# Weight pieces of three FFNs at many places in their tiles, and two FFNs with moving rows read and PSUM written from the end

## The chip, the cores and the metric

The kernel runs on one core of a Trainium2 chip. The metric is the time of one execution on the device in microseconds. The core has a matrix engine (TensorE: PE for matmuls, PEld for loading the stationary weights), a vector engine (DVE), a scalar engine (ACT), GpSimd (POOL), and a queue on SyncE (SP) from which the loads from memory are issued. Operands lie in SBUF, with 128 partitions; matmul results go to PSUM.

## What is computed

A two-layer encoder trunk on one sequence of 256 tokens with 1024 features in float32. Each layer is a half-step SwiGLU feed-forward (FFN), a mixing step of windowed attention and a convolution module with gates, a second half-step FFN, and a gated per-layer embedding:

```python
def swiglu(x, w_in, w_out):
    gate, up = jnp.split(x @ w_in, 2, axis=-1)
    return (jax.nn.silu(gate) * up) @ w_out

for i in range(DEPTH):                       # DEPTH = 2
    h = x + 0.5 * swiglu(rms_norm(x, norm_ffn1[i]), w_ffn1_in[i], w_ffn1_out[i])
    u = rms_norm(h, norm_mix[i])
    q, k, v, c, g = jnp.split(u @ w_in[i], splits, axis=-1)
    ...
    h = h + (g_attn * y_attn + g_conv * y_conv) @ w_o[i]
    h = h + 0.5 * swiglu(rms_norm(h, norm_ffn2[i]), w_ffn2_in[i], w_ffn2_out[i])
    x = h + (p[i] @ w_pe_proj[i]) * jax.nn.sigmoid(rms_norm(h, norm_pe[i]) @ w_pe_gate[i])
```

The FFN width is 2816, so `w_ffn*_in` is 1024 x 5632 and `w_ffn*_out` is 2816 x 1024. There are four FFNs; the text numbers them 0 and 1 (first and second of layer 0), 2 and 3 (first and second of layer 1).

## The kernel before

All activations are kept with features on the partitions and the 256 tokens along the free dimension: `x32` and the normed copies are 8 chunks of 128 features by 256 tokens, `h` in the FFN is 22 such chunks. A float32 product is made from three matmuls in a reduced format (float32r): each operand is split into a high and a low part, and high x high, high x low and low x high are accumulated in PSUM. That is the inner loop `mm3`: for each chunk of 128 features of the contraction there are three matmuls, with a 128 x 128 piece of the weights as stationary operand (`w_hi` or `w_lo`) and a 128 x 256 chunk of activations as moving operand.

An FFN first runs `gate_up` 22 times: two output blocks of 128 features (one of the gate, one of the up half), each from 8 chunks, into the PSUM tile `ps_gu`; then `down` 8 times, each from 22 chunks in three groups of 8, 7 and 7, into `ps_fo`. In the trace the operands are named after their tiles: `x0h`/`x0l` are the inputs of FFN 0, `xf0`, `xn0` and `xf1` those of FFNs 1, 2 and 3, and `h_hi`/`h_lo` the hidden rows of each.

The class `Weights` streams the weights in the order in which they are used. `spec` notes one piece, `load_upto` issues its load from memory into a ring of 5 `raw` tiles (8 KiB per partition), and `prep_upto` splits it: ACT copies the high part into a `w_hi` tile (L108) and DVE subtracts it from the raw values into `w_lo` (L109). There are 7 tiles of each, and 6 pieces are made ahead (`LOOK`). `get` hands out the next piece and advances the preparation. The order on each engine comes from a scheduler that reads the program in this order.

The tiles' addresses are set by the order of the pools and by small filler tiles:

```python
ROW = 64
G0, G1, G2 = 24, 16, 8
PLACE = 4
...
def rows(pool, k, name, **kw):
    t = pool.tile([P, k * T + ROW], F32R, name=name, **kw)
    return t[:, PLACE : PLACE + k * T].rearrange("p (k t) -> p k t", t=T)
```

With these the 4 KiB `w_hi` and `w_lo` tiles begin at multiples of 256 bytes within a partition (the first of them at 64768), and every tile of moving rows begins 112 bytes past one (`x0h` at 130400 + 16, `h_hi` at 162144 + 16). A piece of weights is a run of 128 elements for each chunk, 512 bytes apart; a chunk of rows is 1024 bytes. So in each FFN matmul the moving operand lies 112 bytes behind the stationary one, modulo 256.

Two small products of the mixing step, `keys_values` (`ps_kv`, L733 to L735) and `queries` (`ps_q`, L777 to L779), have the roles exchanged: 128 tokens of the rows are stationary and the weights move, 256 or 512 columns at a time. `attn_out` (`ps_ao`, L946) multiplies in full float32 from the raw tiles.

Of the kernel before, what the change touches and what calls it, by code (L numbers as in the profile page):

```python
# [10 lines left out]
F32R = mybir.dt.float32r  # L11
# [4 lines left out]
P = 128  # L16
T = 256
D = 1024
KD = D // P
# [4 lines left out]
QD = 512  # L24
CD = 512
KC = CD // P
# [6 lines left out]
NEG = -1e9  # L33
LOOK = 6
RAW_BUFS = 5
DMA_SCRATCH = 8192
BACKGROUND = 800
WEIGHTS_LAG = 100
ATTN = 7
# [2 lines left out]
ROW = 64  # L42
G0, G1, G2 = 24, 16, 8
PLACE = 4


class Weights:


# [2 lines left out]
    def __init__(self, tc, raw_pool, w_pool):  # L52
        self.tc, self.nc = tc, tc.nc
        self.raw_pool, self.w_pool = raw_pool, w_pool
        self.units, self.specs = [], []
        self.raw, self.ready, self.held, self.hooks = {}, {}, {}, []
        self.next_load = self.next_prep = self.next_get = 0
        self.behind = ()
        self.rest, self.pin, self.lag, self.parts = 0, None, 0, 1

    def unit(self, k, n, sources):
        self.units.append((k, n, sources))
        return len(self.units) - 1

    def spec(self, k, n, pieces):

        self.specs.append((k, n, pieces, False))

    def raw_spec(self, unit, k, c0, n):
        self.specs.append((k, n, [(unit, 0, c0, 0, n)], True))  # L70

    def limit(self):
        held = [p[0] for s in self.specs[self.next_get : self.next_prep] if s[3] for p in s[2]]
# [12 lines left out]
    def prep_upto(self, i):  # L86
        nc = self.nc
        while self.next_prep <= min(i, len(self.specs) - 1):
            k, n, pieces, as_is = self.specs[self.next_prep]
            for u, *_ in pieces:  # L90
                self.load_upto(u + RAW_BUFS - 2)
                if u >= self.next_load:
                    return
            if as_is:
                ((u, k0, s0, _, w),) = pieces
                self.ready[self.next_prep] = self.raw[u][:, k0 : k0 + k, s0 : s0 + w]
                self.next_prep += 1
                continue
            hi = self.w_pool.tile([P, KD * P], F32R, name="w_hi")
            lo = self.w_pool.tile([P, KD * P], F32R, name="w_lo")  # L100
            hv = hi[:, : k * n].rearrange("p (k n) -> p k n", n=n)
            lv = lo[:, : k * n].rearrange("p (k n) -> p k n", n=n)
            step = k // self.parts
            for a, (u, k0, s0, d0, w) in ((a, p) for a in range(0, k, step) for p in pieces):
                at = slice(a, a + step)
                src = self.raw[u][:, k0 + a : k0 + a + step, s0 : s0 + w]
                parts = (
                    nc.scalar.copy(out=hv[:, at, d0 : d0 + w], in_=src),  # L108
                    nc.vector.tensor_tensor(  # L109
                        out=lv[:, at, d0 : d0 + w],  # L110
                        in0=src,
                        in1=hv[:, at, d0 : d0 + w].bitcast(F32),
                        op=ALU.subtract,
                    ),
                )
                if self.pin:
                    for ins in parts:
                        self.pin(ins)
                    self.pin = None
            self.ready[self.next_prep] = (hv, lv)  # L120
            self.next_prep += 1
# [16 lines left out]
    def get(self):  # L138
        i = self.next_get
        due = [fn for at, fn in self.hooks if at <= i]  # L140
        self.hooks = [h for h in self.hooks if h[0] > i]
        for fn in due:
            fn()
        p0 = self.tc.cur_priority
        self.tc.cur_priority = p0 + self.lag
        with ExitStack() as queue:
            for ins in self.behind:
                queue.enter_context(self.tc.issue_after(ins))
            self.prep_upto(i + LOOK - self.rest)
        self.tc.cur_priority = p0  # L150
        self.next_get += 1
        return self.ready.pop(i)


@with_exitstack
def encoder_kernel(ctx: ExitStack, tc: tile.TileContext, a: dict, out: bass.AP):
    nc = tc.nc
# [71 lines left out]
    ws = Weights(tc, raw_pool, w_pool)  # L229
# [4 lines left out]
    def cols_unit(w, k, c0, n):  # L234
        return ws.unit(k, n, [(whole, w[: k * P, c0 : c0 + n].rearrange("(k p) n -> p k n", p=P))])

    def ffn_specs(w_in, w_out, quick=False):
        for j in range(KF // 2):
            if quick and j == 0:
                for c in range(2):  # L240
                    for c0 in (0, FF):
                        u = cols_unit(w_in, KD, c0 + c * P, P)
                        ws.spec(KD, P, [(u, 0, 0, 0, P)])
                continue
            ug = cols_unit(w_in, KD, j * 256, 256)
            uu = cols_unit(w_in, KD, FF + j * 256, 256)
            for c in range(2):
                ws.spec(KD, P, [(ug, 0, c * P, 0, P)])
                ws.spec(KD, P, [(uu, 0, c * P, 0, P)])
        for f in range(KD // 2):  # L250
            us = [
                ws.unit(n, 256, [(whole, w_out[k0 * P : (k0 + n) * P, f * 256 : (f + 1) * 256].rearrange("(k p) n -> p k n", p=P))])
                for k0, n in KGROUPS
            ]
            for c in range(2):
                for u, (_, n) in zip(us, KGROUPS):
                    ws.spec(n, P, [(u, 0, c * P, 0, P)])

    KGROUPS = [(0, 8), (8, 7), (15, 7)]

    def mix_specs(l):
        w = a["w_in"][l]
        c0 = QD + 2 * P

        def conv_specs(j, n):
            uv = cols_unit(w, KD, c0 + j * P, n * P)
            ug = cols_unit(w, KD, c0 + CD + j * P, n * P)
            for c in range(n):
                ws.spec(KD, P, [(uv, 0, c * P, 0, P)])
                ws.spec(KD, P, [(ug, 0, c * P, 0, P)])  # L270

        conv_specs(0, 2)
        ukv = cols_unit(w, KD, QD, 256)
        for i in range(2):
            ws.spec(KC, 256, [(ukv, i * KC, 0, 0, 256)])
        for i in range(2):
            uq = cols_unit(w[i * KC * P : (i + 1) * KC * P], KC, 0, QD)
            for k in range(0, KC, 2):
                ws.spec(2, QD, [(uq, k, 0, 0, QD)])
        conv_specs(2, 2)  # L280
        g0 = QD + 2 * P + 2 * CD
        for j in range(8):
            u = cols_unit(w, KD, g0 + j * 256, 256)
            for c in range(2):
                ws.spec(KD, P, [(u, 0, c * P, 0, P)])
        w = a["w_attn_out"][l]
        for j in range(2):
            src = w[:, j * 512 : (j + 1) * 512].rearrange("(v c p) n -> v p c n", v=2, p=HD)
            u = ws.unit(KC, 512, [
                (lambda v: v[0:HD], src[0]),  # L290
                (lambda v: v[HD : 2 * HD], src[1]),
            ])
            for c in range(2):
                ws.raw_spec(u, KC, c * 256, 256)
        w = a["w_conv_out"][l]
        for j in range(2):
            u = cols_unit(w, KC, j * 512, 512)
            for c in range(2):
                ws.spec(KC, 256, [(u, 0, c * 256, 0, 256)])
        w = a["w_o"][l]  # L300
        for j in range(4):
            u = cols_unit(w, KD, j * 256, 256)
            for c in range(2):
                ws.spec(KD, P, [(u, 0, c * P, 0, P)])

    def pe_specs(l):
        up = cols_unit(a["w_pe_proj"][l], 2, 0, 1024)
        for c in range(2):
            ws.spec(2, 512, [(up, 0, c * 512, 0, 512)])
        for j in range(4):  # L310
            u = cols_unit(a["w_pe_gate"][l], KD, j * 256, 256)
            for c in range(2):
                ws.spec(KD, P, [(u, 0, c * P, 0, P)])

    for l in range(L):
        ffn_specs(a["w_ffn1_in"][l], a["w_ffn1_out"][l], quick=l == 0)
        mix_specs(l)
        ffn_specs(a["w_ffn2_in"][l], a["w_ffn2_out"][l])
        pe_specs(l)


# [10 lines left out]
    def mm3(ps, w, x, first=True, last=True, k0=0, x_k0=0, n_k=None, cols=slice(0, P), pin=False):  # L332
        (wh, wl), (xh, xl) = w, x
        n_k = wh.shape[1] if n_k is None else n_k
        for k in range(n_k):
            kx = x_k0 + k
            f, e = first and k == 0, last and k == n_k - 1
            for wa, xa, a, b in ((wh, xh, f, False), (wh, xl, False, False), (wl, xh, False, e)):
                mm = nc.tensor.matmul(ps, wa[:, k0 + k, cols], xa[:, kx, :], start=a, stop=b)  # L339
                if pin:  # L340
                    tc.keep_in_program_order(mm)

# [153 lines left out]
    with tc.manual_schedule(engines={mybir.EngineType.Activation, mybir.EngineType.DVE}):  # L496
# [9 lines left out]
        for k in range(KD):  # L506
            if 2 <= k < 6:
                xT[k] = mm_tile("ps_xt")[:, :T]
            else:
                c0 = 0 if k < 2 else 512  # L510
# [712 lines left out]
```

## Time and profile before

| | us |
|---|---|
| median of 2 runs | 1093.14 |
| the runs | 1092.87, 1093.42 |
| the profiled execution | 1092.97 |
| its span, first to last instruction | 1091.2 |
| FFN 0, first ps_gu to last ps_fo | 9.7 to 192.5 |
| FFN 1 | 339.4 to 519.9 |
| FFN 2 | 547.6 to 727.7 |
| FFN 3 | 874.6 to 1055.2 |

The profiled execution is 1.8 us longer than its span, and 0.2 us under the median. In the page's rows a busy time is the union of an engine's instructions; matmuls overlap one another, so that the mean duration of one says little of how fast they follow each other. A view by tile gives minimum, median and maximum duration in ns, and the starts of the first and the last of a group in us. The granted clock of TensorE was 0.998 of full speed over the span.

### The profile page before, as it was taken

The numbers are of one execution on the slowest core, as the hardware profiler recorded it, in microseconds if no ns is written. First come the engines' busy times: TensorE is split into PE (matmuls) and PEld (weight loads), VectorE is DVE, ScalarE is ACT, GpSimd is POOL, SyncE is SP. The second block draws the span as 40 slices with busy tenths as digits, with TensorE's granted clock in tenths as the row PEclk, the third lists the DMA queues.
The fourth block names the chain that finished last, engine by engine and source line by source line (L and its number), as shares of the span: only waits on it lengthen the run. The fifth ranks groups of instructions, "written<-read, shape, count | busy, mean of one in ns | idle before, by whom it ended". The sixth has DMA issues, their size and how long they took to land.

```text
span 1091.2 us, 22048 instructions
## 1 busy us (share of the span) xinstructions
PE 1082.8 (99%) x9178; PEld 1061.2 (97%) x9178; DVE 822.0 (75%) x1229; ACT 621.0 (57%) x1040; POOL 84.5 (8%) x123
## 2 busy tenths in 40 slices
PE   9999999999999999999999999999999999999997
PEld 9999999999999999999999999999998999999997
DVE  6876666899989766666886666669999986666664
ACT  7655445676767555445765554557776665554552
POOL 2000001210002000001100000113100100000110
PEclk9999999999999999999999999999999999999999
DMA  9876556556066646546556564566634666564531
GB/s 310 281 250 220 179 166 226 177 170 178 15 230 231 220 166 219 182 167 232 185 177 216 171 210 148 186 229 195 154 117 139 212 200 216 172 207 148 188 115 39
DMA packets 195695, 203.01 MB, mean 186 GB/s; under 512 B 3731, under 2 KB 188899, under 8 KB 195596
## 3 DMA queue, kind: packets, MB, share of 16 engines
q1 hardware_dynamic: 195564, 201.60, 55.9%
q8 instruction: 72, 1.18, 0.4%
q14 instruction: 27, 0.22, 0.1%
q10 hardware_dynamic: 32, 0.01, 0.0%
HBM read 200.53 MB, written 1.06 MB: 185 GB/s over the span
## 4 chain that ended last, share of the span: by engine, by line
PE 92%; DVE 2%; ACT 2%; DMA 1%; issue 1%; POOL 0%; SPq 0%; DVEq 0%; ACTq 0%; POOLq 0%
PE ps_gu L339 41%; PE ps_fo L339 22%; PE ps_g L339 8%; PE ps_c L339 4%; PE ps_pe L339 4%; PE ps_wo L339 4%; PE ps_co L1049 2%; DMA raw<-in_w_ffn_in_dram 1%; DVE w_lo L109 1%; PE ps_pp L339 1%; PE ps_s L818 1%; ACT g L932 1%; PE ps_o L874 1%; PE ps_q L778 1%; PE ps_q L777 1%
## 5 line engine op out<-in xcount | busy, mean ns | idle before, releaser
L109 DVE TENSOR_TENSOR w_lo<-raw,w_hi 128x1024 fp32r<-128x1024 f32 (+2 forms) x377 | 450.9, 1202 | 199.3 <-ACT w_hi L108 199.3
L108 ACT CAST w_hi<-raw 128x1024 fp32r<-128x1024 f32 (+2 forms) x377 | 387.7, 1034 | 365.1 <-PE ps_gu L339 191.0
L339 PE MATMUL ps_fo<-h_hi,w_hi 128*128 128x256 f32 x704 | 193.0, 275 | 0.0
L339 PE MATMUL ps_fo<-h_lo,w_hi 128*128 128x256 f32 x704 | 193.0, 275 | 0.0
L339 PE MATMUL ps_fo<-h_hi,w_lo 128*128 128x256 f32 x704 | 193.0, 275 | 0.0
L339 PEld LDWEIGHTS ps_fo<-h_lo,w_hi 128*128 128x128 f32 x704 | 131.8, 188 | 0.0
L339 PEld LDWEIGHTS ps_fo<-h_hi,w_lo 128*128 128x128 f32 x704 | 131.8, 188 | 0.0
L339 PEld LDWEIGHTS ps_fo<-h_hi,w_hi 128*128 128x128 f32 x704 | 131.8, 188 | 0.0
L443 POOL TENSOR_TENSOR sq_acc<-sq_acc,sq 128x256 f32<-128x256 f32 x56 | 52.6, 939 | 829.2 <-ACT sq L442 828.8
L669 DVE SCALAR_TENSOR_TENSOR y<-cpad,cw,y 128x256 f32<-128x256 f32 x240 | 101.8, 487 | 0.1
L339 PE MATMUL ps_gu<-xf0l,w_hi 128*128 128x256 f32 x352 | 97.0, 276 | 0.0
L339 PE MATMUL ps_gu<-xf1l,w_hi 128*128 128x256 f32 x352 | 97.0, 276 | 0.0
L339 PE MATMUL ps_gu<-xn0h,w_hi 128*128 128x256 f32 x352 | 97.0, 276 | 0.0
L339 PE MATMUL ps_gu<-xf0h,w_hi 128*128 128x256 f32 x352 | 96.9, 275 | 0.0
L339 PE MATMUL ps_gu<-xf1h,w_hi 128*128 128x256 f32 x352 | 96.9, 275 | 0.0
L339 PE MATMUL ps_gu<-xf0h,w_lo 128*128 128x256 f32 x352 | 96.9, 275 | 0.0
L339 PE MATMUL ps_gu<-xf1h,w_lo 128*128 128x256 f32 x352 | 96.9, 275 | 0.0
L339 PE MATMUL ps_gu<-xn0h,w_lo 128*128 128x256 f32 x352 | 96.8, 275 | 0.0
L339 PE MATMUL ps_gu<-xn0l,w_hi 128*128 128x256 f32 x352 | 96.8, 275 | 0.0
L339 PE MATMUL ps_gu<-x0h,w_lo 128*128 128x256 f32 x336 | 92.8, 276 | 0.2 <-DVE w_lo L109 0.2
L339 PE MATMUL ps_gu<-x0h,w_hi 128*128 128x256 f32 x336 | 92.9, 276 | 0.0
L339 PE MATMUL ps_gu<-x0l,w_hi 128*128 128x256 f32 x336 | 92.5, 275 | 0.0
(243 smaller groups left out, 2690.4 us busy)
## 6 DMA issues: line engine op xcount, KB each, us to landing
raw<-in_w_ffn_in_dram SPq DMA_DIRECT2D x86, 1024.0 KB
raw<-in_w_in_dram SPq DMA_DIRECT2D x30, 1024.0 KB
raw<-in_w_ffn_out_dram SPq DMA_DIRECT2D x32, 896.0 KB
raw<-in_w_ffn_out_dram SPq DMA_DIRECT2D x16, 1024.0 KB
raw<-in_w_o_dram SPq DMA_DIRECT2D x8, 1024.0 KB
raw<-in_w_pe_gate_dram SPq DMA_DIRECT2D x8, 1024.0 KB
raw<-in_w_attn_out_dram SPq DMA_DIRECT2D x8, 512.0 KB
raw<-in_w_conv_out_dram SPq DMA_DIRECT2D x4, 1024.0 KB
```

The source lines that it names most:

```text
L108: nc.scalar.copy(out=hv[:, at, d0 : d0 + w], in_=src),
L109: nc.vector.tensor_tensor(out=lv[:, at, d0 : d0 + w], in0=src, in1=hv[:, at, d0 : d0 + w].bitcast(F32), op=ALU.subtract,),
L339: mm = nc.tensor.matmul(ps, wa[:, k0 + k, cols], xa[:, kx, :], start=a, stop=b)
L443: nc.gpsimd.tensor_tensor(out=self.acc, in0=self.acc, in1=sq, op=ALU.add)
L669: last_tap[0] = nc.vector.scalar_tensor_tensor(out=y[:, i, :], in0=src, scalar=w, in1=y[:, i, :], op0=ALU.mult, op1=ALU.add)
L777: nc.tensor.matmul(o_, u[0][:, kx, ts], wh[:, k, :], start=kx == 0, stop=False)
L778: nc.tensor.matmul(o_, u[0][:, kx, ts], wl[:, k, :], start=False, stop=False)
L818: mm = nc.tensor.matmul(ps[v][:, c, :], qT[v * HD : (v + 1) * HD, c, qb * P : (qb + 1) * P], kT[v * HD : (v + 1) * HD, :], start=True, sto ...
L874: mm = nc.tensor.matmul(ps[v * HD : (v + 1) * HD, :], vt[:, b, v * HD : (v + 1) * HD], pT[v][:, b, :], start=b == 0, stop=b == 1,)
L932: tc.keep_in_program_order(nc.scalar.activation(out=gs, in_=gs, func=AF.Sigmoid))
L1049: mm = nc.tensor.matmul(ps[:, c, :], wa[:, k, c * P : (c + 1) * P], ya[:, k, :], start=(i, k) == (0, 0), stop=(i, k) == (2, KC - 1),)
```

## The change

Weight pieces can now begin at a place other than the start of their tile, and matmuls of a piece can run in one of two directions.

- `PLACES` lists for FFNs 1, 2 and 3 how many bytes the moving rows are to lie behind the weights, modulo 256: 11 values for the pieces of `w_in` (4 pieces in a row share one) and 4 for those of `w_out` (6 share one). For FFN 1 these are 92 to 132 in steps of 4, and 188 to 200 in steps of 4. For FFNs 2 and 3 they are multiples of 8 over the whole ring, FFN 3 between those of FFN 2. `place_of` turns a value into a place, `(112 - behind) % 256 // 4` elements from the tile's start; 112 would give place 0.
- FFNs 2 and 3 get the direction `BACK`: both the moving rows and the PSUM columns of a matmul are given with step -1, so that column 255 is read and written first. The result is the same. `Weights.get` sets the direction of the piece it hands out in `way`, and `mm3` uses it. FFN 1 keeps `ON`, step 1.
- The pieces of `ps_kv` get place 12 (48 bytes) and those of `ps_q` place 32 (128 bytes), in both layers.
- The `w_hi` and `w_lo` tiles are 64 elements (256 bytes) longer, 14 x 256 = 3584 bytes per partition in all; `DMA_SCRATCH`, the memory set aside per partition for DMA, goes from 8192 to 4096 bytes to make room. Tiles still begin at multiples of 256 bytes (the first `w_hi` at 60672), and the rows still 112 past one.
- FFN 0 and all other pieces keep place 0 and direction `ON`.

The instructions, their shapes and their order are the same row by row on all five engines; what differs is the addresses of the weight pieces and, in layer 1's FFNs, the sign of the step in two operands.

```diff
-DMA_SCRATCH = 8192
+DMA_SCRATCH = 4096
...
+ON, BACK = slice(None, None, 1), slice(None, None, -1)
+PLACES = {
+    1: ((92, 96, 100, 104, 108, 112, 116, 120, 124, 128, 132), (188, 192, 196, 200), ON),
+    2: ((0, 16, 32, 48, 64, 80, 96, 112, 128, 144, 160), (176, 192, 208, 224), BACK),
+    3: ((240, 8, 24, 40, 56, 72, 88, 104, 120, 136, 152), (168, 184, 200, 232), BACK),
+}
+
+def place_of(number, outer, piece):
+    if number not in PLACES:
+        return 0, ON
+    inner_, outer_, way = PLACES[number]
+    behind = outer_[piece // 6] if outer else inner_[piece // 4]
+    return (112 - behind) % 256 // 4, way
...
-            hi = self.w_pool.tile([P, KD * P], F32R, name="w_hi")
-            lo = self.w_pool.tile([P, KD * P], F32R, name="w_lo")
-            hv = hi[:, : k * n].rearrange("p (k n) -> p k n", n=n)
-            lv = lo[:, : k * n].rearrange("p (k n) -> p k n", n=n)
+            hi = self.w_pool.tile([P, KD * P + ROW], F32R, name="w_hi")
+            lo = self.w_pool.tile([P, KD * P + ROW], F32R, name="w_lo")
+            hv = hi[:, place : place + k * n].rearrange("p (k n) -> p k n", n=n)
+            lv = lo[:, place : place + k * n].rearrange("p (k n) -> p k n", n=n)
...
         self.next_get += 1
+        self.way = self.ways.get(i, ON)
         return self.ready.pop(i)
...
-                ws.spec(KD, P, [(ug, 0, c * P, 0, P)])
-                ws.spec(KD, P, [(uu, 0, c * P, 0, P)])
+                ws.spec(KD, P, [(ug, 0, c * P, 0, P)], *place_of(number, False, n_in))
+                ws.spec(KD, P, [(uu, 0, c * P, 0, P)], *place_of(number, False, n_in + 1))
+                n_in += 2
...
-                    ws.spec(n, P, [(u, 0, c * P, 0, P)])
+                    ws.spec(n, P, [(u, 0, c * P, 0, P)], *place_of(number, True, n_out))
+                    n_out += 1
...
-            ws.spec(KC, 256, [(ukv, i * KC, 0, 0, 256)])
+            ws.spec(KC, 256, [(ukv, i * KC, 0, 0, 256)], 12)
...
-                ws.spec(2, QD, [(uq, k, 0, 0, QD)])
+                ws.spec(2, QD, [(uq, k, 0, 0, QD)], 32)
...
-                mm = nc.tensor.matmul(ps, wa[:, k0 + k, cols], xa[:, kx, :], start=a, stop=b)
+                mm = nc.tensor.matmul(ps[:, ws.way], wa[:, k0 + k, cols], xa[:, kx, ws.way], start=a, stop=b)
```

More of the change, by code (lines that the diff above doesn't have):

```diff
@@ L54, in __init__ @@
         self.raw_pool, self.w_pool = raw_pool, w_pool
-        self.units, self.specs = [], []
+        self.units, self.specs, self.ways = [], [], {}
         self.raw, self.ready, self.held, self.hooks = {}, {}, {}, []
@@ L59, in __init__ @@
         self.rest, self.pin, self.lag, self.parts = 0, None, 0, 1
+        self.way = ON
     def unit(self, k, n, sources):
@@ L63, in unit, with spec @@
         return len(self.units) - 1
-    def spec(self, k, n, pieces):
-        self.specs.append((k, n, pieces, False))
+    def spec(self, k, n, pieces, place=0, way=ON):
+        self.specs.append((k, n, pieces, False, place))
+        self.ways[len(self.specs) - 1] = way
     def raw_spec(self, unit, k, c0, n):
-        self.specs.append((k, n, [(unit, 0, c0, 0, n)], True))
+        self.specs.append((k, n, [(unit, 0, c0, 0, n)], True, 0))
     def limit(self):
@@ L88, in prep_upto @@
         while self.next_prep <= min(i, len(self.specs) - 1):
-            k, n, pieces, as_is = self.specs[self.next_prep]
+            k, n, pieces, as_is, place = self.specs[self.next_prep]
             for u, *_ in pieces:
@@ L235, in cols_unit, with ffn_specs @@
         return ws.unit(k, n, [(whole, w[: k * P, c0 : c0 + n].rearrange("(k p) n -> p k n", p=P))])
-    def ffn_specs(w_in, w_out, quick=False):
+    def ffn_specs(w_in, w_out, number, quick=False):
+        n_in = n_out = 0
         for j in range(KF // 2):
@@ L315, in encoder_kernel @@
     for l in range(L):
-        ffn_specs(a["w_ffn1_in"][l], a["w_ffn1_out"][l], quick=l == 0)
+        ffn_specs(a["w_ffn1_in"][l], a["w_ffn1_out"][l], 2 * l, quick=l == 0)
         mix_specs(l)
-        ffn_specs(a["w_ffn2_in"][l], a["w_ffn2_out"][l])
+        ffn_specs(a["w_ffn2_in"][l], a["w_ffn2_out"][l], 2 * l + 1)
         pe_specs(l)
```

## The prediction

> **What bounds the kernel now.** I read the page first: busy shares, slices and the chain of waits.
>
> ```profile
> span 1091.2 us, 22048 instructions
> PE 1082.8 (99%) x9178; PEld 1061.2 (97%) x9178; DVE 822.0 (75%) x1229; ACT 621.0 (57%) x1040; POOL 84.5 (8%) x123
> PEclk9999999999999999999999999999999999999999
> PE 92%; DVE 2%; ACT 2%; DMA 1%; issue 1%; POOL 0%; SPq 0%; DVEq 0%; ACTq 0%; POOLq 0%
> ```
>
> TensorE is busy in every slice at full clock and is 92% of the chain. The next view, who waited for whom on PE, shows whether anything feeds it late.
>
> ```profile
> PE ps_out L1132 <- DVE x L1121: 1.6, 1, 1.6
> PE ps_warm L190 <- POOL ones_d L183: 1.1, 1, 1.1
> PE ps_yc L991 <- DVE yn L978: 0.5, 2, 0.3
> PE ps_gu L348 <- ACT w_hi L108: 0.5, 1, 0.5
> PE ps_gu L339 <- DVE w_lo L109: 0.2, 1, 0.2
> ```
>
> These waits sum to 3.9 us of 1091. So the kernel's time is the number of matmuls times the distance between their starts (the cadence), and the change can only act through that. The durations in the groups are of no use for it, since matmuls overlap. I take cadences from first start, last start and count in the view by tile (min/median/max in ns, then the two starts in us).
>
> ```profile
> L339 PE MATMUL ps_gu<-xn0l,w_hi x352: 275/275/281, 547.8 to 667.6; 128*128 128x256 f32 x176
> L339 PE MATMUL ps_fo<-h_lo,w_hi x176: 275/275/275, 460.2 to 519.7; 128*128 128x256 f32 x176
> L735 PE MATMUL ps_kv<-w_hi,xm0l x16: 277/283/289, 204.5 to 209.9; 128*128 128x256 f32 x16
> L779 PE MATMUL ps_q<-w_hi,xm0l x16: 390/394/394, 210.5 to 221.0; 128*128 128x512 f32 x16
> ```
>
> Each row is one of three matmuls that alternate. ps_fo: (519.7 - 460.2) / (3 x 175) = 113.3 ns. ps_gu: (667.6 - 547.8) / (3 x 351) = 113.8 ns, with a few other matmuls in between. ps_kv, with as many columns: 5.4 / 45 = 120.0 ns. ps_q, 512 columns: 10.5 / 45 = 233.3 ns, or 116.7 per 256. What differs is the distance of the two operands. In all FFN matmuls of before the moving rows begin 112 bytes past a multiple of 256 and the weights at a multiple. In ps_kv and ps_q the roles are exchanged, so the moving operand begins 112 bytes before the stationary one (144 modulo 256). The durations say what happens: 275 ns is the shortest of any of these 256-column matmuls and ps_fo never leaves it, while ps_kv varies around 283. I read this as the moving stream being held up by the reading of the next weights, at some distances and not at others. That is my inference from two distances.
>
> A second sign is the start of the kernel, at the good distance (timeline: start, us, instruction).
>
> ```profile
> 9.70 1.26 PE L348 MATMUL ps_gu<-x0h,w_hi 128*128 128x256 f32 x8 [0.51 <-ACT w_hi L108]
> 10.80 1.10 PE L348 MATMUL ps_gu<-x0l,w_hi 128*128 128x256 f32 x8
> 11.74 1.07 PE L348 MATMUL ps_gu<-x0h,w_lo 128*128 128x256 f32 x8
> 12.64 1.07 PE L348 MATMUL ps_gu<-x0h,w_hi 128*128 128x256 f32 x8
> 13.55 1.07 PE L348 MATMUL ps_gu<-x0l,w_hi 128*128 128x256 f32 x8
> ```
>
> The eight from 10.80 to 11.74 take 117.5 ns each, the later eights 113. So even at 112 the stream has two states: a disturbed one of 117 to 118 ns, and a steady one of 113 which it finds after about a dozen matmuls and then keeps. ps_kv never finds it in 48.
>
> **The change part by part.** No engine's order of instructions changes; only addresses and directions do.
>
> Amount of work. An FFN has 3 x 352 matmuls of ps_gu and 3 x 176 of ps_fo, 1584. FFN 1 (second of layer 0) is forward at distances of 92 to 132 and 188 to 200 bytes; FFNs 2 and 3 (layer 1) are backward, 3168 matmuls, at distances around the whole ring of 256. FFN 0 stays.
>
> Price of a disturbed matmul over 113.3: 117.5 - 113.3 = 4.2 ns (start) to 120.0 - 113.3 = 6.7 ns (ps_kv). I take 5.5, the middle, since each is one sample of the same state.
>
> FFNs 2 and 3. No matmul of before reads or writes backward, so the share of disturbed ones has to be bounded. From below: nothing, if backward streams stay steady at every distance. From above: all at 6.7 ns, 21.2 us. Of the two forward distances that the trace shows, one is steady, and that one needs a dozen matmuls to become so; for places all round the ring I take three quarters disturbed: 2376 x 5.5 ns = +13.1 us. No cover exists, since PE is the bound.
>
> FFN 1. Places within 20 bytes of 112 are near the steady row, the 188 to 200 group is not near any. Bounds 0 and 1584 x 6.7 = 10.6 us; I take a quarter disturbed, 396 x 5.5 = +2.2 us.
>
> ps_kv and ps_q get other distances (192 and 16), 96 matmuls each. Their best is a stream without stalls: 113.3 for ps_kv, and for 512 columns the next row.
>
> ```profile
> 290.43 7.07 PE L946 MATMUL ps_ao<-o,raw 128*128 128x256 f32 x32
> 297.33 1.04 PE L968 MATMUL ps_yt<-ident,y 128*128 128x128 f32 x8
> ```
>
> 32 records of ps_ao in 6.90 us are 215.6 ns, and taken as two streams of 256 columns (full float32) they are the nearest thing to 512 columns without a stall. So the best is 96 x 6.7 + 96 x 17.7 ns = 2.3 us gained; the other end is as much lost. I take -1.0 us.
>
> Changes of place. FFNs 1 to 3 have 15 places each; if each costs the dozen disturbed matmuls of the start, 45 x 12 x 4.2 ns = 2.3 us, else 0; most are inside the shares above, so +0.5 us.
>
> Writing the pieces. ACT and DVE write w_hi and w_lo at offsets that need not be multiples of 16 bytes.
>
> ```profile
> L109 DVE TENSOR_TENSOR w_lo<-raw,w_hi 128x1024 fp32r<-128x1024 f32 (+2 forms) x377 | 450.9, 1202 | 199.3 <-ACT w_hi L108 199.3
> L108 ACT CAST w_hi<-raw 128x1024 fp32r<-128x1024 f32 (+2 forms) x377 | 387.7, 1034 | 365.1 <-PE ps_gu L339 191.0
> L669 DVE SCALAR_TENSOR_TENSOR y<-cpad,cw,y x240: 395/484/512, 209.7 to 830.5; 128x256 f32<-128x256 f32 x120
> 548.00:668.00 120.00, 120.00 (x1059) 119.94 (x1058) 86.57 (x114) 64.79 (x96) 1.94 (x3) 1.00 0.56 186
> ```
>
> The convolution taps (L669) read at every 4-byte offset in turn, and their longest is 6% over the median: bounds 0 and 6% for reads, and I take it for writes too. DVE is busy 86.6 of 120 us in the first half of FFN 2 (last row: PE, PEld, DVE, ACT, POOL) and ACT 64.8, so 6% stays hidden: 0. That cover would be gone at some 40% more per piece; then PE would wait on w_lo. ACT's idle time before a piece ends with PE freeing a slot, so pieces are made ahead of need.
>
> DMA scratch halved: 0. Nearly all bytes (201.60 of 203.01 MB) move in one hardware queue, at 55.9% of the 16 engines' span:
>
> ```profile
> q1 hardware_dynamic: 195564, 201.60, 55.9%
> ```
>
> The pieces' preparation waits for slots rather than for these loads (the L108 row), which is the cover; without it each late load would show as a wait of PE on w_hi or w_lo, and 0.7 us is all there is of that now.
>
> Sum: 13.1 + 2.2 - 1.0 + 0.5 = +14.8 us. The profiled execution took 1092.97 us (span 1091.2 plus 1.8 around it), 0.2 below the median of 1093.14. 1092.97 + 14.8 = 1107.8, rounded to 1108 us. Its own range goes from half of the backward matmuls at 4.2 ns and nothing else, 3168 / 2 x 4.2 = 6.7 us (1099), to all at 6.7 with FFN 1's quarter at 6.7 (2.7 us) and 2.3 of changes, +26 us (1119).
>
> **The rivals.**
> 1. Places hardly matter: a steady state exists at nearly every distance and both ways. For it: ps_fo holds 113.3 through all its places in memory. Against: ps_kv. Time: -2.3 (kv, q) to +5 us, some 1091 to 1098. [...]
> 2. Backward streams are held up more, because the two readings meet instead of following each other. The nearest price is the worst stall that a row shows: ps_q, 233.3 - 215.6 = 17.7 ns per weight load. 3168 x 17.7 = 56 us, 1149 us.
> 3. Backward reading or PSUM writing runs at half rate: the moving 256 columns then take what ps_ao takes. 3168 x (215.6 - 113.3) = 324 us, about 1417 us. Against it, ACT reads PSUM backward in two places at the usual cost (L882 reversed, L489 pT_h not, same size):
>
> ```profile
> L882 ACT COPY o<-ps_o 128x512 f32<-128x512 f32 x4 | 2.3, 587 | 11.5 <-PE ps_o L874 11.5
> L489 ACT CAST pT_h<-ps_pt 128x512 fp32r<-128x512 f32 x2 | 1.2, 578 | 0.0
> ```
>
> That is another engine, and reading. [...]
> 4. The other side, faster: 113.3 itself contains a stall that some distance removes. ps_ao's half is 107.8 ns; 5.5 ns x 4752 matmuls would be 26 us, 1067, if every place were free, and it decides for faster over 2% only if more than 84% of them are (21.9 / 26). Against it: no 256-column row has a duration under 275, and the steady rows sit on it, so I see no stall left there.
>
> **How the numbers follow.** A measurement of this kernel can tell about 2% (21.9 us) from no change: slower begins at 1115, faster ends at 1071. Chances: the forecast 0.45, rival 1 0.28, rival 2 0.14, rival 3 0.08, rival 4 0.05. Of the forecast a quarter lies over 1115 (0.10); with rivals 2 (0.13) and 3 (0.08) slower has 0.31. Faster gets 0.02 of rival 4. Same keeps 0.67. The range takes in the forecast, rival 1 and the lower part of rival 2: 1090 to 1140, which leaves out rival 3, half of rival 2 and most of rival 4, 0.19.
>
> **What would show it.** Right: ps_fo and ps_gu of layer 1 at several cadences between 113 and 121 ns, changing with the place, medians of duration at 280 to 285; FFN 0 unchanged at 113.3; PE still without waits. Layer 1's FFNs, 120 and 60 us each by the windows now, would last some 186 us each. Wrong: layer 1's FFNs at 113.3 throughout (rival 1), at 131 (rival 2) or over 200 (rival 3); any 256-column row with starts under 112 ns apart (rival 4); or PE waiting on w_lo, which would mean the writes of the pieces have become the bound.

## The result and the profile after

| us | before | after |
|---|---|---|
| median | 1093.14 (2 runs) | 1118.92 (2 runs) |
| the runs | 1092.87, 1093.42 | 1118.82, 1119.03 |
| the profiled execution | 1092.97 | 1119.03 |
| its span | 1091.2 | 1117.2 |

The ratio is 1.0232, with a 95% interval of 1.0214 to 1.0251: slower by 2.3%, 26 us. The forecast was 1108 us in a range of 1090 to 1140, with "within 2%" as the likeliest class; the time lies in the range and just past that line.

The page of the kernel after, in the same lines as those shown of before:

```profile
span 1117.2 us, 22050 instructions
PE 1109.3 (99%) x9178; PEld 1087.8 (97%) x9178; DVE 821.8 (74%) x1229; ACT 620.5 (56%) x1040; POOL 85.9 (8%) x123
PEclk9999999999999999999999999999999999999999
PE 87%; DVE 8%; ACT 2%; POOL 1%; issue 1%; DMA 1%; SPq 0%; ACTq 0%; DVEq 0%; POOLq 0%
```

The span grew by 26.0 us and PE's busy time by 26.5, with the same 9178 matmuls at full clock (granted 1.000 over the span). DVE and ACT are busy as long as before. Who waited for whom on PE:

```profile
PE ps_out L1154 <- DVE x L1143: 1.6, 1, 1.6
PE ps_warm L209 <- POOL ones_d L202: 1.1, 1, 1.1
PE ps_yc L1013 <- DVE yn L1000: 0.5, 2, 0.3
PE ps_gu L370 <- ACT w_hi L126: 0.3, 1, 0.3
```

3.5 us, against 3.9 before. So nothing feeds PE late; the matmuls themselves follow each other more slowly. The views by tile give where (min/median/max duration in ns, then first and last start in us; ps_fo once for each FFN in turn). First the groups of before that the prediction did not need:

```profile
L339 PE MATMUL ps_gu<-xf0l,w_hi x352: 275/275/471, 339.5 to 459.9; 128*128 128x256 f32 x176
L339 PE MATMUL ps_gu<-xf1l,w_hi x352: 275/275/471, 874.7 to 995.1; 128*128 128x256 f32 x176
L339 PE MATMUL ps_fo<-h_lo,w_hi x176: 275/275/275, 667.9 to 727.4; 128*128 128x256 f32 x176
L339 PE MATMUL ps_fo<-h_lo,w_hi x176: 275/275/275, 995.4 to 1054.9; 128*128 128x256 f32 x176
```

Then the same groups after, and ps_kv and ps_q of layer 0:

```profile
L361 PE MATMUL ps_gu<-xf0l,w_hi x352: 275/282/467, 339.2 to 464.6; 128*128 128x256 f32 x176
L361 PE MATMUL ps_gu<-xn0l,w_hi x352: 279/283/287, 554.9 to 681.6; 128*128 128x256 f32 x176
L361 PE MATMUL ps_gu<-xf1l,w_hi x352: 279/282/468, 891.9 to 1018.3; 128*128 128x256 f32 x176
L361 PE MATMUL ps_fo<-h_lo,w_hi x176: 275/275/275, 132.6 to 192.1; 128*128 128x256 f32 x176
L361 PE MATMUL ps_fo<-h_lo,w_hi x176: 275/279/289, 465.0 to 526.8; 128*128 128x256 f32 x176
L361 PE MATMUL ps_fo<-h_lo,w_hi x176: 279/284/284, 682.0 to 744.8; 128*128 128x256 f32 x176
L361 PE MATMUL ps_fo<-h_lo,w_hi x176: 279/282/283, 1018.7 to 1080.9; 128*128 128x256 f32 x176
L757 PE MATMUL ps_kv<-w_hi,xm0l x16: 275/275/275, 204.4 to 209.5; 128*128 128x256 f32 x16
L801 PE MATMUL ps_q<-w_hi,xm0l x16: 387/392/398, 210.0 to 220.3; 128*128 128x512 f32 x16
```

From first to last start, in us (before's FFN 2 ps_gu and FFN 1 ps_fo are in the prediction's rows):

| | ps_gu before | ps_gu after | ps_fo before | ps_fo after | together |
|---|---|---|---|---|---|
| FFN 1, forward | 120.4 | 125.4 | 59.5 | 61.8 | +7.3 |
| FFN 2, backward | 119.8 | 126.7 | 59.5 | 62.8 | +10.2 |
| FFN 3, backward | 120.4 | 126.4 | 59.5 | 62.2 | +8.7 |

These are +26.2 us, the whole of the loss. ps_kv took 5.1 us where it took 5.4, and ps_q 10.3 where it took 10.5, so with layer 1 some -1.0. Most of that does not reach the end of the stage: from the last ps_fo row of FFN 2 to the first ps_gu row of FFN 3 it takes 891.9 - 744.8 = 147.1 us after, and took 874.7 - 727.4 = 147.3 before; why is not shown. FFN 0 is untouched: ps_fo 59.5 us, all at 275 ns.

The busy counts in windows of 10 us within single places of FFN 1's ps_gu show how sharply places differ (us; PE busy and matmuls that touch the window, the other engines, clock, DMA share, GB/s; the places are 96, 100, 108, 112 and 116 bytes):

```profile
351.50:361.50 10.00, 10.00 (x86) 10.00 (x85) 7.15 (x10) 5.11 (x9) 0.00 (x0) 1.00 0.75 248
363.00:373.00 10.00, 10.00 (x90) 10.00 (x90) 7.04 (x10) 5.28 (x9) 0.00 (x0) 1.00 0.65 211
386.00:396.00 10.00, 10.00 (x86) 10.00 (x85) 6.50 (x8) 4.60 (x8) 0.00 (x0) 1.00 0.64 211
397.00:407.00 10.00, 10.00 (x90) 10.00 (x90) 6.93 (x9) 5.13 (x8) 0.00 (x0) 1.00 0.62 210
408.00:418.00 10.00, 10.00 (x85) 10.00 (x85) 6.47 (x9) 5.00 (x8) 0.00 (x0) 1.00 0.63 211
```

At 112 and 100 some four matmuls more fit into the same time than at 108, 96 and 116. From the starts of all matmuls of a place (the distances between starts sorted, the shortest and the longest tenth left out, and the mean of the rest; so for every cadence below that has no row) come: 112, 113.3 ns; 100, 113.5; 192, 113.3; and 117.2 to 120.2 at the twelve other places of FFN 1. In FFN 2, 10 of the 11 ps_gu places lie at 120.0, and no place of the two backward FFNs is under 117.7. A place at 113.3 is called steady below, any other disturbed.

### The profile page after: what moved, and what is told of

Same layout as the page of the kernel before. It is cut to its first block, busy times and chain, and to the rows that moved or that the text cites. A ratio compares the mean times of both kernels' runs of the same rounds, so it can differ in the third digit from the quotient of the medians.

```text
span 1117.2 us, 22050 instructions
## 1 busy us (share of the span) xinstructions
PE 1109.3 (99%) x9178; PEld 1087.8 (97%) x9178; DVE 821.8 (74%) x1229; ACT 620.5 (56%) x1040; POOL 85.9 (8%) x123
## 3 DMA queue, kind: packets, MB, share of 16 engines
q1 hardware_dynamic: 195564, 201.60, 54.7%
## 4 chain that ended last, share of the span: by engine, by line
PE 87%; DVE 8%; ACT 2%; POOL 1%; issue 1%; DMA 1%; SPq 0%; ACTq 0%; DVEq 0%; POOLq 0%
PE ps_gu L361 44%; PE ps_fo L361 22%; PE ps_pe L361 4%; PE ps_wo L361 4%; PE ps_g L361 4%; DVE y L691 4%; PE ps_c L361 2%; PE ps_co L1071 2%; DVE w_lo L127 2%; PE ps_pp L361 1%; DMA raw<-in_w_ffn_in_dram 1%; PE ps_ao L968 1%; DVE s L857 1%; ACT w_hi L126 1%; PE ps_s L840 0%
## 5 line engine op out<-in xcount | busy, mean ns | idle before, releaser
L127 DVE TENSOR_TENSOR w_lo<-raw,w_hi 128x1024 fp32r<-128x1024 f32 (+2 forms) x377 | 451.0, 1202 | 213.2 <-ACT w_hi L126 213.2
L126 ACT CAST w_hi<-raw 128x1024 fp32r<-128x1024 f32 (+2 forms) x377 | 386.7, 1032 | 390.2 <-PE ps_gu L361 208.6
L361 PE MATMUL ps_fo<-h_hi,w_lo 128*128 128x256 f32 x704 | 196.5, 280 | 0.0
L361 PE MATMUL ps_fo<-h_lo,w_hi 128*128 128x256 f32 x704 | 196.4, 280 | 0.0
L361 PE MATMUL ps_fo<-h_hi,w_hi 128*128 128x256 f32 x704 | 196.4, 280 | 0.0
L361 PE MATMUL ps_gu<-xn0h,w_hi 128*128 128x256 f32 x352 | 99.8, 284 | 0.0
L361 PE MATMUL ps_gu<-xn0h,w_lo 128*128 128x256 f32 x352 | 99.6, 283 | 0.0
L361 PE MATMUL ps_gu<-xn0l,w_hi 128*128 128x256 f32 x352 | 99.6, 283 | 0.0
L361 PE MATMUL ps_gu<-xf1l,w_hi 128*128 128x256 f32 x352 | 99.5, 283 | 0.0
L361 PE MATMUL ps_gu<-xf1h,w_hi 128*128 128x256 f32 x352 | 99.4, 282 | 0.0
L361 PE MATMUL ps_gu<-xf1h,w_lo 128*128 128x256 f32 x352 | 99.2, 282 | 0.0
```

What stands on the lines that cost most here:

```text
L127: nc.vector.tensor_tensor(out=lv[:, at, d0 : d0 + w], in0=src, in1=hv[:, at, d0 : d0 + w].bitcast(F32), op=ALU.subtract,),
L361: mm = nc.tensor.matmul(ps[:, ws.way], wa[:, k0 + k, cols], xa[:, kx, ws.way], start=a, stop=b)
```

## The experiments

All diffs are against the kernel after, with `...` where lines are left out. Each kernel was run once, beside the kernel before on the same chip, except where an interval is given. The theories have letters in the expectations: D says that the distance of the operands alone decides, L that the rows' start within 16 bytes counts too, S that it is the rows' start within 32 bytes together with the distance.

**All distances, forward.** Every FFN runs forward, over 49 distances that the kernel after does not use forward, with ten repeats of those that it does; ps_kv and ps_q get further distances too.

```diff
...
+    0: ((0, 4, 8, 12, 16, 20, 24, 28, 32, 36), (232, 236, 240, 244), ON),
+    1: ((40, 44, 48, 52, 56, 60, 64, 68, 72, 76, 80), (248, 252, 112, 192), ON),
+    2: ((84, 88, 136, 140, 144, 148, 152, 156, 160, 164, 168), (100, 108, 96, 120), ON),
+    3: ((172, 176, 180, 184, 204, 208, 212, 216, 220, 224, 228), (104, 128, 196, 200), ON),
...
```

> All four FFNs forward, over the 49 distances (multiples of 4 bytes, modulo 256) that the changed kernel did not visit, with ten known ones repeated at other places of the program; ps_kv and ps_q visit twelve distances. Theory D (the distance from the next weights to the moving rows sets the cadence, and only few narrow distances are steady): the repeats come out as in the changed kernel (100, 112 and 192 at 113 to 114 ns; 96, 104, 108, 120, 128, 196, 200 at 117 to 121), and some 10 of the 49 new ones are steady, the share of 3 in 15 seen so far; time about 1093 + 0.8 x 6336 x 6 ns = 1123 us. Rival (forward is good nearly everywhere and the 12 disturbed places of FFN 1 are an exception round 112): over half of the 49 at 113 to 114 ns, time under 1110 us. Rival (the stage or the tile decides, not the distance): the repeats differ from their first values by more than 2 ns.

Measured: 1122.88 us (before, on the same chip, 1092.63). The views by tile within three places, 112 in ps_fo, 44 and 216 in ps_gu:

```profile
L366 PE MATMUL ps_fo<-h_lo,w_hi x44: 275/275/275, 503.9 to 518.6; 128*128 128x256 f32 x44
L366 PE MATMUL ps_gu<-xf0l,w_hi x33: 276/282/288, 357.9 to 369.4; 128*128 128x256 f32 x33
L366 PE MATMUL ps_gu<-xf1l,w_hi x32: 275/275/283, 977.1 to 987.7; 128*128 128x256 f32 x32
```

Of the 49 new distances only two were steady, 40 and 216, where ten had been expected; the others lie at 116.6 to 121.6 ns. The ten repeats came out as in the kernel after (within 0.2 ns), eight of them in another FFN and seven in the other product. So a distance's state is repeatable, and with this start of the rows five of 64 forward distances are steady: 40, 100, 112, 192 and 216. They are single points: 108 and 116 on both sides of 112 are disturbed (120.0 and 120.1 ns in the kernel after).

**Both operands moved together.** All rows and all pieces begin 36 bytes later; every distance and direction is as in the kernel after.

```diff
-PLACE = 4
+PLACE = 13
...
-        return 0, ON
+        return 9, ON
...
-    return (112 - behind) % 256 // 4, way
+    return (148 - behind) % 256 // 4, way
...
```

> The changed kernel with the moving rows and all weight pieces 36 bytes further on, so that each distance and direction is kept and every address modulo 16, 32 and 256 is another one. Theory D: each place keeps its cadence (FFN 1: 113 to 114 ns at 100, 112 and 192, 117 to 120 elsewhere; FFNs 2 and 3 117 to 122; FFN 0 113.3), time within 2 us of the 1118.9 us of the changed kernel. Rival (the alignment of the weight piece or of the rows itself decides): FFN 0 at 112 leaves 113.3 for 117 to 120, worth 7 to 10 us, and the good places of FFN 1 move.

Measured: 1157.30 us. FFN 0 at 112 and FFN 2 backward (ps_fo):

```profile
L361 PE MATMUL ps_fo<-h_lo,w_hi x176: 283/287/289, 141.3 to 205.5; 128*128 128x256 f32 x176
L361 PE MATMUL ps_fo<-h_lo,w_hi x176: 282/282/282, 709.7 to 772.7; 128*128 128x256 f32 x176
```

Theory D fell. At the same distance of 112 bytes FFN 0 went from 113.3 to 64.2 / 525 = 122.3 ns, and 100 and 192 are disturbed as well (120.7, 118.8). So where the two operands start counts too, and not their distance alone. Backward stayed at 63.0 / 525 = 120.0, so here too nothing was steady.

**The two directions apart.** All FFNs at 112. FFN 2 reads the rows backward and writes PSUM forward, FFN 3 the reverse. In both the 256 columns come out in reversed order and no later step turns them back, so this kernel does not compute the trunk and serves for its times alone.

```diff
...
+    1: ((112,) * 11, (112,) * 4, ON),
+    2: ((112,) * 11, (112,) * 4, (ON, BACK)),
+    3: ((112,) * 11, (112,) * 4, (BACK, ON)),
...
+                wr, rd = ws.way if isinstance(ws.way, tuple) else (ws.way, ws.way)
+                mm = nc.tensor.matmul(ps[:, wr], wa[:, k0 + k, cols], xa[:, kx, rd], start=a, stop=b)
```

> All FFNs at distance 112. FFN 2 reads the moving rows forward and writes PSUM backward? No: the pair is (PSUM, rows), so FFN 2 writes PSUM forward and reads the rows backward, FFN 3 writes PSUM backward and reads the rows forward; in both the columns of the products come out in reversed order, which no later step undoes. Theory D with direction of reading: FFN 2 at 118 to 121 ns (about 10 us more than 181 us), FFN 3 at 113.3 (as before), time about 1093 + 10 = 1103 us. Rival (writing PSUM backward is what disturbs): FFN 3 at 118 to 121, FFN 2 at 113.3, also about 1103 us. Rival (only both together, or any single one, does it): both at 113.3 (1092 us) or both at 118 to 121 (1113 us).

Measured: 1101.75 us (before 1092.63). FFN 2's two products, then FFN 3's:

```profile
L362 PE MATMUL ps_gu<-xn0l,w_hi x352: 278/284/286, 546.6 to 673.4; 128*128 128x256 f32 x176
L362 PE MATMUL ps_fo<-h_lo,w_hi x176: 284/284/284, 673.7 to 736.7; 128*128 128x256 f32 x176
L362 PE MATMUL ps_gu<-xf1l,w_hi x352: 275/275/471, 883.5 to 1003.9; 128*128 128x256 f32 x176
L362 PE MATMUL ps_fo<-h_lo,w_hi x176: 275/275/275, 1004.2 to 1063.7; 128*128 128x256 f32 x176
```

Reading the rows backward at 112 costs 63.0 / 525 = 120.0 ns for each matmul; writing PSUM backward costs nothing (59.5 / 525 = 113.3, and ps_gu's 120.4 us as in before). FFN 2's 126.8 + 63.0 us are 10.5 over before; with the 1.0 us that ps_kv and ps_q give back that is 9.5, and 9.1 was measured.

**Backward over the rest of the ring.** The backward FFNs get 34 further distances, so that with the kernel after all 64 multiples of 4 have been read backward; ps_kv and ps_q get others as well.

```diff
...
+    1: ((4, 12, 20, 28, 36, 44, 52, 60, 68, 76, 84), (92, 100, 108, 116), BACK),
+    2: ((124, 132, 140, 148, 156, 164, 172, 180, 188, 196, 204), (212, 220, 228, 236), BACK),
+    3: ((244, 252, 216, 248, 112, 192, 100, 64, 0, 32, 96), (160, 200, 40, 152), BACK),
...
```

> FFNs 1, 2 and 3 backward, over the 34 distances that the changed kernel did not visit backward, with eleven repeats. Theory D in its strict form (a backward stream is disturbed at every distance): all at 117 to 122 ns, time about 1093 + 4752 x 6 ns = 1121 us. Rival (backward has narrow steady distances too, which multiples of 8 missed): some of the 32 distances at 4 modulo 8 at 113 to 114 ns, each worth 96 x 6 ns = 0.6 us.

Measured: 1119.92 us (before 1092.63). FFN 3's ps_fo, at 160, 200, 40 and 152:

```profile
L365 PE MATMUL ps_fo<-h_lo,w_hi x176: 280/282/285, 1019.4 to 1081.8; 128*128 128x256 f32 x176
```

None of the distances is steady; all lie at 117.7 to 120.0 ns, also 40, 100, 112, 192 and 216, which are steady forward.

**One bad distance among three.** A triple takes its weights from w_hi twice and from w_lo once. Here w_hi and w_lo get different distances, one steady (112) and one disturbed (108).

```diff
...
+HI_LO = {1: (112, 108), 2: (108, 112), 3: (108, 108)}
...
+            ph, pl = place if isinstance(place, tuple) else (place, place)
+            hv = hi[:, ph : ph + k * n].rearrange("p (k n) -> p k n", n=n)
+            lv = lo[:, pl : pl + k * n].rearrange("p (k n) -> p k n", n=n)
```

> All forward. FFN 1: high pieces at the steady distance 112, low pieces at 108 (120.0 ns in the changed kernel); FFN 2 the other way round; FFN 3 both at 108; FFN 0 both at 112. The weights of a matmul are read while the one before it streams. Theory D (a matmul is held up by the reading of the next weights): in FFN 1 the matmul that streams while a low piece is read (low rows with high weights) is the long one, 280 ns and more, and the two others stay at 275; three in a row take 340 to 350 ns instead of 340 (steady) or 360 (both at 108), so FFN 1 is 0 to 5 us longer than before and FFN 3 10.6 us longer. Rival (a matmul is held up by its own weights): the long one is high rows with low weights. Rival (steadiness is a state of the whole stream, and one bad distance in three breaks it): all three at 280 to 285 ns, FFNs 1 and 2 as long as FFN 3.

Measured: 1115.50 us (before 1092.92). FFN 1's ps_fo, where only w_lo is at the bad distance:

```profile
L356 PE MATMUL ps_fo<-h_hi,w_hi x169: 277/281/287, 465.3 to 524.7; 128*128 128x256 f32 x169
L356 PE MATMUL ps_fo<-h_lo,w_hi x169: 279/280/285, 465.4 to 524.8; 128*128 128x256 f32 x169
L356 PE MATMUL ps_fo<-h_hi,w_lo x169: 278/281/286, 465.6 to 524.9; 128*128 128x256 f32 x169
```

All three are longer than 275, and their starts follow at 116.7 to 118.3 ns. It is not the one matmul beside the bad weights that is held up; one bad distance in three takes the whole stream out of its steady state. FFN 2, with the two w_hi matmuls at 108 and the w_lo one at 112, came to 118.7 in both products. FFN 3, with both at 108, came to 117.7 to 118.1, where 108 gave 120.0 in the kernel after: the size of a disturbed value, as against whether it is disturbed, also depends on something else than the place.

**Rows and pieces moved by powers of two.** Everything forward at 112; each product's rows and weights move together by a number of bytes of its own.

```diff
...
+X_ON = {"x0": 16, "xf0": 8, "xn0": 1, "xf1": 3}
+H_ON = (4, 12, 2, 32)
...
-        return t[:, PLACE : PLACE + k * T].rearrange("p (k t) -> p k t", t=T)
+        at = PLACE + X_ON.get(name[:-1], on)
+        return t[:, at : at + k * T].rearrange("p (k t) -> p k t", t=T)
```

> All forward, all at distance 112; rows and weights are moved on together by another amount in each product: ps_gu of FFNs 0 to 3 by 64, 32, 4 and 12 bytes, ps_fo of FFNs 0 to 3 by 16, 48, 8 and 128. The run with both moved by 36 bytes left 113.3 for 122.3 ns, so the distance alone does not decide. Theory L (the moving rows must start at a multiple of 16 bytes): 113.3 ns where the move is 16, 32, 48, 64 or 128, and 120 to 123 where it is 4, 8 or 12; time about 1092 + (1056 + 1056 + 528) x 8 ns = 1113 us. Rival (32 bytes): 16 and 48 also disturbed, 1120 us. Rival (64 bytes): only 64 and 128 steady, 1128 us. Rival (absolute places modulo 256 or more): none steady, 1140 us.

Measured: 1117.27 us (before 1092.92). Moved by 32 bytes (xf0), by 4 (xn0), and ps_fo by 16 (FFN 0) and by 128 (FFN 3):

```profile
L355 PE MATMUL ps_gu<-xf0l,w_hi x352: 274/275/468, 342.0 to 462.3; 128*128 128x256 f32 x176
L355 PE MATMUL ps_gu<-xn0l,w_hi x352: 283/287/288, 553.8 to 682.9; 128*128 128x256 f32 x176
L355 PE MATMUL ps_fo<-h_lo,w_hi x176: 282/283/283, 132.2 to 195.2; 128*128 128x256 f32 x176
L355 PE MATMUL ps_fo<-h_lo,w_hi x176: 274/275/290, 1019.6 to 1079.2; 128*128 128x256 f32 x176
```

| moved by | 4 | 8 | 12 | 16 | 32 | 48 | 64 | 128 |
|---|---|---|---|---|---|---|---|---|
| ns | 122.3 | 124.4 | 116.4 | 120.0 | 113.3 | 120.0 | 113.3 | 113.3 |

At this distance of 112 it is steady at multiples of 32 bytes and disturbed at 16 and 48: the period is 32, not 16, and theory L fell. The 4-byte move gives 122.3, as the 36-byte move above did. Theory S, distance plus the rows' start within 32 bytes, came out of this. At one distance the weights' start moves with the rows', so it cannot be told which of the two starts is the one that counts.

**Only ps_kv and ps_q.** The FFNs forward at 112 as before; the longer tiles and the halved DMA memory stay, and both mixing products are at 192.

```diff
-    if number not in PLACES:
...
+    return 0, ON
...
-                ws.spec(2, QD, [(uq, k, 0, 0, QD)], 32)
+                ws.spec(2, QD, [(uq, k, 0, 0, QD)], 12)
```

> All FFNs as before the change, forward at distance 112; ps_kv keeps the changed kernel's place (distance 192, 113.3 ns against 120.0) and ps_q goes to distance 192 too (226.6 ns in the scan against 233.3). Theory D: 96 x 6.7 + 96 x 6.7 ns = 1.3 us less than before, ratio 0.9988; with it, the longer weight tiles and the halved DMA scratch cost nothing. Rival (they cost something): 1.000 or more.

**Everything at 192.** As the last, with all other pieces at the other steady distance.

```diff
+    return 44, ON
...
-    def spec(self, k, n, pieces, place=0, way=ON):
+    def spec(self, k, n, pieces, place=44, way=ON):
```

> As the run before, but every other piece lies at distance 192 instead of 112. Theory D: 192 is as steady as 112 (113.3 ns in ps_fo), so within 1 us of the run before (ratio 0.998 to 0.999 to before). Rival (steady states differ in how soon they are found after a pause of TensorE): ps_g, ps_c and ps_pe, whose mean is 116 to 117 ns, change by up to 1 ns, 2 us in all.

Measured, medians of 11 runs: with only ps_kv and ps_q changed 1092.00 us, ratio to before 0.9994 (0.9986 to 1.0003); with everything at 192 1091.72, ratio 0.9990 (0.9981 to 0.9999); before 1092.92 on the same chip. ps_kv and ps_q of the one with everything at 192:

```profile
L746 PE MATMUL ps_kv<-w_hi,xm0l x16: 275/275/275, 204.0 to 209.1; 128*128 128x256 f32 x16
L790 PE MATMUL ps_q<-w_hi,xm0l x16: 392/392/393, 209.7 to 220.0; 128*128 128x512 f32 x16
```

Longer tiles and the smaller DMA memory cost nothing that can be measured. The kernel with everything at 192 is the fastest one run, 1.2 us under before, about what ps_kv and ps_q give; its interval only just leaves out no change, and the two kernels' intervals overlap, so no gain from a sooner steady state is shown.

**Another start of the rows, forward.** Rows at a multiple of 32 bytes instead of 16 past one, and 59 of the 64 forward distances.

```diff
-PLACE = 4
+PLACE = 8
...
...
+    0: ((0, 8, 16, 24, 32, 36, 40, 44, 48, 52), (192, 196, 200, 204), ON),
...
-        return 0, ON
+        return 4, ON
...
-    return (112 - behind) % 256 // 4, way
+    return (128 - behind) % 256 // 4, way
...
```

> All rows moved on by 16 bytes, so that they begin at a multiple of 32 (128 modulo 256); all FFNs forward, over 59 distances; every other piece at distance 112, which moving both by 16 bytes left at 120.0 ns. Theory S (the state is set by the start of the moving rows modulo 32 together with the distance to the weights): the steady set is another one than 40, 100, 112, 192 and 216; as many, some 5 of 59, and none under 113 ns; what was 113.3 in ps_g, ps_c, ps_pe and ps_wo (1728 matmuls) is 120; time about 1092 + 6336 x 0.92 x 5.8 + 1728 x 6 ns = 1136 us. Rival (only rows at 16 modulo 32 can be steady): none of 59 steady, 1140 us. Rival (the steady distances stay where they were): 40, 100, 192 and 216 at 113.3.

Measured: 1133.03 us (before 1092.79). Places 192 and 196 in ps_fo, 168 in ps_gu, 216 in ps_fo:

```profile
L362 PE MATMUL ps_fo<-h_lo,w_hi x44: 276/276/276, 136.4 to 151.0; 128*128 128x256 f32 x44
L362 PE MATMUL ps_fo<-h_lo,w_hi x45: 276/281/293, 151.0 to 166.8; 128*128 128x256 f32 x45
L362 PE MATMUL ps_gu<-xf1l,w_hi x32: 276/276/278, 964.8 to 975.4; 128*128 128x256 f32 x32
L362 PE MATMUL ps_fo<-h_lo,w_hi x44: 279/282/286, 506.2 to 521.6; 128*128 128x256 f32 x44
```

Steady are 52, 168, 180, 192 and 204; of the old five 40, 100 and 216 are now disturbed, as 112 is after the 16-byte move above, and only 192 remains. Theory S held (it had given 1136 us): the list of good distances belongs to one start of the rows within 32 bytes.

**Other starts, backward.** Backward with the rows of ps_gu at a multiple of 32 (33 distances) and those of ps_fo 8 past one (12 distances).

```diff
-PLACE = 4
+PLACE = 8
...
...
+    1: ((0, 8, 16, 24, 32, 40, 48, 56, 64, 72, 80), (4, 24, 44, 64), BACK),
+    2: ((88, 96, 104, 112, 120, 128, 136, 144, 152, 160, 168), (84, 104, 124, 144), BACK),
+    3: ((176, 184, 192, 200, 208, 216, 224, 232, 240, 248, 116), (164, 184, 204, 224), BACK),
...
+    return ((136 if outer else 128) - behind) % 256 // 4, way
...
+        return t[:, PLACE + on : PLACE + on + k * T].rearrange("p (k t) -> p k t", t=T)
...
+        h = tuple(rows(hp, KF, "h_" + part, on=2 * ((l, gain_name) != (0, "norm_mix"))) for part in ("hi", "lo"))
```

> FFNs 1 to 3 backward with the rows at two other starts modulo 32: 0 for ps_gu (33 distances) and 8 for ps_fo (12 distances). Theory S with reading backward always disturbed: all at 117 to 123 ns, as at 16 (64 distances) and 20 (30 distances). Rival (backward has steady places too, at another start of the rows): some at 113.3 ns.

Measured: 1142.09 us (before 1092.79). FFN 0, forward at 112 from the new start, is disturbed as well (120.0) and has its part in that time. FFN 1's ps_fo, at 4, 24, 44 and 64:

```profile
L361 PE MATMUL ps_fo<-h_lo,w_hi x176: 282/282/291, 479.8 to 543.4; 128*128 128x256 f32 x176
```

None is steady; the backward places lie at 117.7 to 123.3 ns. With 64 distances at a start of 16 within 32 bytes and 30 at 20 (the 36-byte move), 139 combinations have been read backward, and not one was steady.

## Why the prediction was right or wrong

The path was right: PE is the bound, it waits for nothing new, and 26.0 us came from the distances between the starts of matmuls, which went from 113.3 to some 120 ns at most places. What was off are the shares of disturbed matmuls (in both terms too low), and the belief that a place near a good one is good.

- **Backward, 13.1 us.** Measured 10.2 + 8.7 = 18.9. The price holds: 18.9 us over 3168 matmuls is 6.0 ns each, within the bounds of 4.2 and 6.7 and near the 5.5 taken. The share fails: "for places all round the ring I take three quarters disturbed" should have read all of them. The term is 5.8 us short: a quarter of the matmuls at 5.5 ns is 4.4 us, the rest is the price.
- **FFN 1, 2.2 us.** Measured 7.3. The step that fails is "Places within 20 bytes of 112 are near the steady row": nearness does not help, in these runs steadiness holds at single distances. 12 of its 15 places are disturbed (117.2 to 120.2 ns), not a quarter. The term is 5.1 us short.
- **ps_kv and ps_q, -1.0 us.** -1.0 by their rows, but only some -0.3 by the stages that they stand in (0.2 us in layer 0 and 0.1 in layer 1, from the last start of ps_fo to the next start of ps_gu).
- **Changes of place, +0.5 us.** From 108 to 112 one matmul is off 113 or 114 ns; coming to 100 about a dozen are. Too small to tell from the rest.
- **Writing the pieces, 0.** The groups of ACT and DVE and the main DMA queue after:

```profile
L127 DVE TENSOR_TENSOR w_lo<-raw,w_hi 128x1024 fp32r<-128x1024 f32 (+2 forms) x377 | 451.0, 1202 | 213.2 <-ACT w_hi L126 213.2
L126 ACT CAST w_hi<-raw 128x1024 fp32r<-128x1024 f32 (+2 forms) x377 | 386.7, 1032 | 390.2 <-PE ps_gu L361 208.6
q1 hardware_dynamic: 195564, 201.60, 54.7%
```

The means of 1202 and 1032 ns (1202 and 1034 before) show that writing at offsets in steps of 4 bytes cost nothing here, so the cover for 6% was not needed. (That cover was also larger than the 40% given: DVE's idle 33.4 us in that window are 62% of the 54.3 us that L109 takes there.) **DMA memory, 0:** the queue's share fell only with the longer span (54.7% of 1117.2 us against 55.9% of 1091.2), and the kernel with ps_kv and ps_q alone changed, which keeps the smaller memory, was no slower than before (1092.00 us against 1092.92).

The terms off by 5.8 and 5.1 us make the miss of 11 us, from 1107.8 to 1119.0 for the profiled execution. The forecast's own range ended at 1119, with all backward matmuls disturbed at the full price: the kernel went to that end, though by other parts. Backward cost 18.9 us where that end has 21.2, and FFN 1 7.3 where it has 2.7; that these parts, with the 2.3 for changes of place, make up for one another is luck. A quarter of the forecast's chance had been put over 1115 us, which is why "within 2%" looked likeliest. The windows to look for were nearly met: layer 1's FFNs last 189.9 and 189.0 us (554.9 to 744.8, 891.9 to 1080.9) where 186 was named, and the medians of duration in their rows are 282 to 284. The cadences change with the place as named, but only from 117.7 to 120.1; none is near 113.

The rivals:

1. Places hardly matter: fell, by 113.3 against 120.0 within one product and one kernel, and by the 36-byte move, in which FFN 0 went from 113.3 to 122.3 ns at the same distance.
2. 17.7 ns more per backward matmul: fell; the worst backward place of any run is 123.3, 10 ns over.
3. Half rate: fell. Writing PSUM backward cost nothing (113.3 ns), and reading backward added at most those 10 ns.
4. A floor under 113.3: no place of any run has a mean below it.

The prediction's reading, "the moving stream being held up by the reading of the next weights, at some distances and not at others", is half right. Distance matters (113.3 ns at 112, 120.0 at 108), and so does where the operands begin within 32 bytes (120.0 at 112 too, once both are moved by 16). That the stationary operand's reading is what holds up the moving one was not shown. The run with w_hi and w_lo apart, where all three matmuls grew (medians of 281, 280 and 281 ns in FFN 1's ps_fo, against 275) and not one of them, speaks against its simplest form: one bad distance in three spoiled the steady state of the whole stream there. What lies beneath, why backward rows were never steady, and what sets a disturbed place's value between 115.5 and 124.4 stay open.

## What to carry to other kernels

Where PE is busy throughout, read the distance between the starts of matmuls, product by product, and compare products of equal shape: here a product some 6% slower than its like (ps_kv, 120.0 ns against 113.3) was held up by where its operands lie, and no view of waits showed that. A good place is a single point here (five of 64 distances at one start of the rows, five of 59 at another), and the neighbours of a good place were as disturbed as others (120.0 and 120.1 ns beside 112); a place once found had to be kept with both operands' starts (the moving one's within 32 bytes, and the distance): moved together by 16 bytes, 112 went from 113.3 to 120.0 ns. In these runs only rows read forward were ever steady (backward they lay at 117.7 to 123.3 ns), and PSUM could be written in either direction (113.3 ns both ways).

## What the runs showed of the chip that was not expected

- With the two directions apart, reading the moving rows with step -1 took 120.0 ns against 113.3 at the same place, while writing PSUM with step -1 cost nothing (ps_fo of FFN 3 in that kernel, 113.3 ns, all at 275 in duration).
- At a distance of 112, the start of the two operands counts with a period of 32 bytes: rows moved together with their weights by 32, 64 or 128 bytes keep 113.3 ns, by 16 or 48 they go to 120.0, by 4, 8 or 12 to 122.3, 124.4 and 116.4.
- In the pairs compared it does not matter whether activations or weights move: ps_kv, whose moving operand is the weights, has nearly the cadence of an FFN product at the same distance and the same start within 32 bytes (FFN products in the forward run over the ring, ps_kv in it at 64 and in the backward one at the others; 0: 118.5 and 118.3; 32: 118.2 and 118.2; 64: 118.4 and 118.3; 128: 120.1 and 119.9; 160: 117.1 and 116.7). Except at 0, the two starts are 32 to 128 bytes apart, modulo 256, so these pairs fit a period of 32 at these distances too.
